# One trunk step on one core: a wider element stage in the RWKV layer, inverses of two head pairs together, and a memory projection in another place

## The chip, the cores and the metric

The kernel runs on one core of one Trainium2 chip. The metric is the device time of one execution in microseconds; the time before is the median of three runs. Its engines are called PE (matmuls; PEld is its weight loading), DVE and ACT (elementwise work that can also read PSUM, where matmul results land), POOL (elementwise work on SBUF only) and SP, whose queue issues nearly all of this kernel's transfers.

## The reference

One step of a two-layer network of width 1024 serves 512 prompt tokens and eight requests of 16 tokens. Layer 0 mixes by pooling and differential attention, layer 1 by RWKV; each is followed by cross attention to a memory of 256 rows and by a SwiGLU. What the change touches is in layer 1:

```python
    xr, xw, xk, xv, xa, xg = [h + xx * mu[i] for i in range(6)]
    r, k, v = xr @ wr, xk @ wk, xv @ wv
    a = jax.nn.sigmoid(a0 + (xa @ a1) @ a2)
    kk = heads(k * k_k)
    kk = kk / jnp.maximum(jnp.sqrt(jnp.sum(kk * kk, axis=-1, keepdims=True)), 1e-12)
    k = k * (1 + (a - 1) * k_a)
    decay = jnp.exp(-jnp.exp(w.astype(f32)))

    def step(S, inp):
        r_t, d_t, k_t, v_t, kk_t, a_t = inp
        sa = jnp.einsum('bhvk,bhk->bhv', S, -kk_t)
        S = (S * d_t[:, :, None, :] + sa[..., None] * (kk_t * a_t)[:, :, None, :]
             + v_t[..., None] * k_t[:, :, None, :])
        return S, jnp.einsum('bhvk,bhk->bhv', S, r_t)
```

Cross attention takes its keys and values from the memory, `mem_prompt @ xa_wk` and `mem_prompt @ xa_wv` (256 x 1024 each), which are also outputs.

## The kernel before, in words

All 640 tokens are columns (two halves of 320). Every large product is done in two-part arithmetic: an operand is split into a high part (a cast, mostly on ACT: `wh`, `split`) and a low part (a subtraction, on DVE or POOL: `wl`), and three matmuls are added. A product is a chain of steps, weights loaded by SP, cast, subtracted, multiplied, evicted from PSUM. Work is written in program order, and a scheduler then sets the order of each engine's instructions from its own estimates; on the chip each engine keeps its order and waits on semaphores. A tile with a tag lives in a ring of as many buffers as it was given, and the next user waits for the last one to be done with the buffer.

`rwkv` (layer 1) runs like this. Ahead of the keys, the memory's keys and values are made from `memhl`, the transposed memory in two parts (`mem_ksteps`, `mem_vsteps`); in the trace K is `p_g<-memhl,wh` and V is `p_g<-wh,memhl`. In the same time ACT, DVE and POOL make the mixed inputs (`mixed`: tiles `mixt`, `mixr`). Then come the key product (`kraw`, through `keep`), the low-rank inputs and the receptances.

The element stage goes over eight head pairs m, two heads on 128 partitions (`elem`, `rw_elem`). For each it makes: the decay's products (tiles `u`, `pi` and the views `P`, `S`); the normed key `kn`; `am`, the in-context rate and later the changed key; `zr`, the two left operands of each of ten chunks (eight of 64 prompt tokens, two of four requests each); `bk`, the two right operands per head, written over zeros in the other head's rows. From these PE makes the masked products `gm` of each chunk (`p_f<-zr,bk`), and transposes of bk (`p_f<-ident,bk`, copied out by ACT into `am`/`pi` tiles that go to DRAM as `d_bt`). zr, gm and their like go to DRAM (`d_w`, `d_gb`) through SP, to come back in another layout. While the head pairs run, pieces of a large product stand between their steps (`pace`: the rate is how many pieces per small PSUM tile; `rest` does all that is left): first the receptances, then the value product.

`inverse` makes, of each head pair, the inverse of a triangular 64 x 64 matrix per chunk: first the 16 x 16 blocks on the diagonal, by a loop of fifteen steps of a product and a sum on DVE (tiles `ix`, `in`, `it`), then a trip through DRAM (`d_np`), then two rounds of small PE products (`p_l`) to the matrix `mt`.

The chunk stage follows the string `CP`: `0` and `1` are the next chunk of the first and of the second half of the head pairs (pairs 0 to 3 and 4 to 7), `s` a sample part, `n` norms, `G` the gate's product, `Y` the last state. A chunk needs the state of the one ahead of it and the inverses of its four head pairs (`p_c<-u,mt`). Then come the gates, the output product, the cross attention of layer 1 (which reads K and V back from DRAM) and its SwiGLU.

## Time and profile before

| what | us |
|---|---|
| median of three runs (lowest, highest) | 2433.68 (2427.9, 2435.51) |
| span of the profiled execution | 2428.2 |
| layer 0, up to the memory projections | 0 to 1024 |
| memory K and V of layer 1, mixing | 1024 to 1096 |
| keys, low-rank inputs, receptances | 1096 to 1230 |
| element stage | 1230 to 1490 |
| chunk stage | 1490 to 1660 |
| norms, gates | 1660 to 1700 |
| output product, cross attention, SwiGLU, final norm | 1700 to 2428 |

The profile shows one execution. The span of 2428.2 us runs from the first to the last recorded instruction; the profiled execution's own time is not listed apart from it, and the median of the runs stands 5.5 us above. The stage borders were read from the first and last instructions of the tiles that belong to each. A row of a tile reads: line, engine, operation, output and inputs by the program's names, count, then shortest, median and longest duration in ns, then the first and last start. A row of a group has in their place the busy time and the mean duration, and, behind the bar, the idle time of the engine just before them and what ended it. A row of a window has its border and length, busy time and count for each engine, then the clock granted to PE as a share of full speed, the busy share of the DMA engines and the GB/s that they moved.

### The profile page before, as it was taken

Reading aid. Unit: us, or ns where it says so; the run is one execution under the profiler, and the core shown is the slowest. Engines: PE = TensorE matmul, PEld = TensorE weight load, DVE = VectorE, ACT = ScalarE, POOL = GpSimd, SP = SyncE. Lnnn points to the kernel's source line nnn. Section 1 sums busy time; section 2 is a strip of 40 time slices with the busy share of each in tenths; the row PEclk is TensorE's granted clock in tenths of the full one; section 3 lists DMA queues with packets and bytes.
Section 4 is the critical chain, followed back from the end, with each engine's and each line's share of the span. In section 5 each row is a group of like instructions: output and inputs, shape, how many; then the busy total and the mean of one; then the engine's idle time right before and its main releaser. Section 6 shows DMA issues by size and latency. Waiting matters only on the chain. (4 is left out here: it accounts for less than half of the span.)

```text
span 2428.2 us, 45754 instructions
## 1 busy us (share of the span) xinstructions
PE 2281.2 (94%) x18943; PEld 2119.8 (87%) x18943; DVE 1284.7 (53%) x2361; ACT 814.5 (34%) x1493; POOL 525.4 (22%) x536
## 2 busy tenths in 40 slices
PE   8998999999999999979998987696999999999998
PEld 7886999789999999978887876574997899999997
DVE  4467543454434424484759886579444544344344
ACT  4335432333212212366734432222323432122122
POOL 2122220012101102244555322233200212011010
PEclk9999999999999999999997878797999999999999
DMA  3218644423222222453245556674445222222222
GB/s 120 74 62 295 204 136 148 160 77 87 74 75 79 71 87 73 135 163 91 74 128 149 145 138 157 183 204 118 135 132 165 65 79 72 77 79 81 76 72 77
DMA packets 428322, 280.42 MB, mean 115 GB/s; under 512 B 79130, under 2 KB 383535, under 8 KB 428114
## 3 DMA queue, kind: packets, MB, share of 16 engines
q1 hardware_dynamic: 424513, 268.01, 38.0%
q0 software_dynamic: 3600, 9.49, 1.1%
q8 instruction: 149, 2.44, 0.4%
q14 instruction: 60, 0.48, 0.1%
HBM read 231.22 MB, written 46.20 MB: 114 GB/s over the span
## 5 line engine op out<-in xcount | busy, mean ns | idle before, releaser
L224 PE MATMUL p_g<-xn,wh 128*128 128x320 f32 x3712 | 721.6, 310 | 0.4 <-DVE xn L208 0.4
L224 PEld LDWEIGHTS p_g<-xn,wh 128*128 128x128 f32 x3712 | 588.7, 188 | 9.8 <-issue 8.4
L241 ACT CAST wh<-wr 128x1024 fp32r<-128x1024 f32 (+3 forms) x279 | 272.8, 978 | 861.7 <-PE p_g L224 534.0
L224 PE MATMUL p_g<-xn,wl 128*128 128x320 f32 x1856 | 444.1, 310 | 3.3 <-DVE wl L205 3.3
L205 DVE TENSOR_TENSOR wl<-wr,wh 128x1024 fp32r<-128x1024 f32 (+2 forms) x251 | 305.6, 1218 | 73.9 <-ACT wh L241 57.2
L224 PEld LDWEIGHTS p_g<-xn,wl 128*128 128x128 f32 x1856 | 316.2, 188 | 7.0 <-DVE wl L205 3.7
L224 PE MATMUL p_g<-hid,wh 128*128 128x320 f32 x1408 | 264.8, 309 | 0.0
L205 POOL TENSOR_TENSOR gate<-gate,sgate 128x320 f32<-128x320 f32 x88 | 118.1, 1363 | 676.1 <-DVE gate L205 517.6
L205 DVE TENSOR_TENSOR gate<-p_g,rstd 128x320 f32<-128x320 f32 x176 | 78.3, 486 | 327.5 <-PE p_g L224 324.8
L205 DVE TENSOR_TENSOR x<-x,p_g 128x320 f32<-128x320 f32 x192 | 85.5, 483 | 281.6 <-PE p_g L224 281.5
L224 PEld LDWEIGHTS p_g<-hid,wh 128*128 128x128 f32 x1408 | 221.4, 188 | 0.0
L224 PE MATMUL p_g<-hid,wl 128*128 128x320 f32 x704 | 161.4, 310 | 0.0
L224 PE MATMUL p_g<-mixr,wh 128*128 128x320 f32 (+2 forms) x640 | 128.4, 313 | 3.1 <-ACT wh L241 2.6
L224 PEld LDWEIGHTS p_g<-hid,wl 128*128 128x128 f32 x704 | 117.6, 188 | 0.0
L224 PE MATMUL p_g<-xohl,wh 128*128 128x320 f32 x512 | 110.0, 319 | 4.8 <-ACT xohl L214 4.7
L224 PEld LDWEIGHTS p_g<-mixr,wh 128*128 128x128 f32 (+2 forms) x640 | 98.5, 179 | 11.6 <-issue 5.6
L205 POOL TENSOR_TENSOR acc<-acc,sq 128x640 f32<-128x640 f32 x36 | 66.2, 1840 | 146.3 <-ACT sq L202 146.1
L224 PEld LDWEIGHTS p_g<-xohl,wh 128*128 128x128 f32 x512 | 82.4, 188 | 9.9 <-ACT xohl L214 7.0
L948 POOL TENSOR_SCALAR xp<-xp,xsm 128x256 f32<-128x256 f32 x32 | 15.3, 478 | 305.6 <-DVE xsm L684 299.6
L224 PE MATMUL p_g<-mixr,wl 128*128 128x320 f32 (+2 forms) x320 | 78.0, 314 | 0.0
L205 POOL TENSOR_TENSOR wl<-wr,wh 128x1024 fp32r<-128x1024 f32 (+2 forms) x28 | 64.4, 2301 | 60.4 <-ACT wh L241 57.2
L205 DVE TENSOR_TENSOR hid<-gate,hid 128x320 fp32r<-128x320 f32 x88 | 72.1, 819 | 7.8 <-ACT hid L214 7.8
(485 smaller groups left out, 3836.4 us busy)
## 6 DMA issues: line engine op xcount, KB each, us to landing
wr<-in_ffn_wg SPq DMA_DIRECT2D x44, 512.0 KB
wr<-in_ffn_wu SPq DMA_DIRECT2D x44, 512.0 KB
kc<-in_cache_mem_k SPq DMA_DIRECT2D x64, 256.0 KB
...
```

Of the source, the lines that this page charges most:

```text
L205: (eng or self.nc.vector).tensor_tensor(out, a, b, op=op)
L224: self.nc.tensor.matmul(out, lhsT, rhs, start=start, stop=stop, **kw)
L241: nc.scalar.copy(wh[0:rows, 0:n], wr[0:rows, 0:n])
L948: nc.gpsimd.tensor_scalar(p, p, rs, 1.0, op0=ALU.mult, op1=ALU.mult)
```

## The change

- Memory V of layer 1 (`mem_vsteps`) no longer stands behind K. It becomes the filler of the chunk stage (`K` at the head of `CP`, rate `KV` = 0.4), `memhl` is built a second time there from `mem_prompt`, and what is left at `G` is done ahead of the gate's product.
- `kn*am` and `am*k` and the `am` products of bk move from POOL to DVE. bk is one pair of tiles of 1280 columns, all ten chunks, in the place of three sets of halves; zr is two such tiles, and is made by four instructions in the place of eight, and stored by two transfers in the place of four.
- `inverse` takes two head pairs at once, after the second of them: its loop has the same thirty instructions for both. Its work tiles `iA` to `iE` have one buffer each and serve both phases. Of the last copies into `mt` two kinds change places between ACT and DVE.
- The low parts of the low-rank weights and `rn` get 128 rows, half of them zeros (`wz`, a tile of rn for each four pairs), where matmuls took 64 rows.
- Slots: 56 for 59; buffers of cached memory values in the cross attention: 8 for 9; POOL's ring of descriptors is smaller.

```diff
-NSLOT = 59
+NSLOT = 56
+BACC = dict(dynamic_dma_scratch_size=4096)
...
-    XV = 9
+    XV = 8
...
-    CP = '01s01sn01s01sn0101Gn01Y01n'
+    CP = 'K01s01sn01s01sn0101Gn01Y01n'
+    KV = 0.4
...
-            if m < 4:
-                rns.append(self.take(1, "rn", dt=F32R))
             a = 16 * m - 48
-            rn = rns[0][0][a:a + 64, 0:NT]
+            rns.append(self.take(1, "rn", dt=F32R))
+            rn = rns[-1][0][a:a + 64, 0:NT]
+            nc.gpsimd.memset(rns[-1][0][64 - a:128 - a, 0:NT].bitcast(F32), 0.0)
...
         with self.scope():
             self.all(self.mem_ksteps(1, self.mem))
-            self.all(self.mem_vsteps(1, self.mem))
         self.give(self.mem)
...
-            f = slice(64 * (m // 4), 64 * (m // 4) + 64)
-            yield from self.rw_elem(m, r, k, rns[0][0][f, 0:NT], selT[m % 4 // 2][0][f, c:c + 128], low_in, sp)
+            yield from self.rw_elem(m, r, k, rns[m // 4][0][:, 0:NT], selT[m % 4 // 2][0][:, c:c + 128], low_in, sp)
             if m < 4:
                 self.give(kr[0][m], kr[1][m])
-            inv[m] = self.inverse(m, sp, nsv[m // 4][:, m % 4])
+            if m % 2:
+                inv[m - 1:m + 1] = self.inverse(m - 1, sp, [nsv[i // 4][:, i % 4] for i in (m - 1, m)])
...
-        bks = self.take(6, "bk")
-        self.bk = [[t[:, 0:NT] for t in bks[2 * i:2 * i + 2]] for i in range(3)]
-        for b in self.bk:
-            for h in range(2):
-                nc.gpsimd.memset(b[h][64 - 64 * h:128 - 64 * h], 0.0)
+        self.bk = [self.wide(f"bk{h}", "bk") for h in range(2)]
+        for h in range(2):
+            nc.gpsimd.memset(self.bk[h][64 - 64 * h:128 - 64 * h], 0.0)
+        wzs = self.take(2, "wz", "n", dt=F32R)
+        self.wz = wzs
+        for t in wzs:
+            nc.gpsimd.memset(t[64:128, 0:128].bitcast(F32), 0.0)
+            nc.gpsimd.memset(t[0:64, 128:256].bitcast(F32), 0.0)
...
+            elif k == "K":
+                self.mem = self.mem_parts("x")
+                with self.inside(crings):
+                    self.pace(self.mem_vsteps(1, self.mem, self.take_tmp()), self.KV)
             elif k == "G":
+                self.rest()
+                self.give(self.mem, self.tmp)
...
-            r = slice(64 * i, 64 * i + 64)
             self.mm(p[:, 0:n], wa[:, i * 128:(i + 1) * 128], low[i][:, t0:t0 + n], start=True, stop=False)
-            self.mm(p[:, 0:n], wa[r, i * 128:(i + 1) * 128], low[2][r, t0:t0 + n], start=False, stop=True)
+            self.mm(p[:, 0:n], wz[:, i * 128:(i + 1) * 128], low[2][:, t0:t0 + n], start=False, stop=True)
...
-        zr = [self.t("zr", 3)[:, 0:NT].rearrange("p (c z t) -> p c z t", c=5, z=2) for _ in range(2)]
-        bk = [[t.rearrange("p (c z t) -> p c z t", c=5, z=2) for t in self.bk[(2 * m + i) % len(self.bk)]] for i in range(2)]
+        v = lambda t: t.rearrange("p (c z t) -> p c z t", c=10, z=2)
+        zr = v(self.wide(f"zr{m % 2}", "zr"))
+        bk = [v(t) for t in self.bk]
         yield
-        self.stt(zr[0][:, :, 0, :], ch(kn[:, 0:320]), -1.0, P[:, 0:5, 0:64])
-        self.stt(zr[1][:, 0:3, 0, :], ch(kn[:, 320:512]), -1.0, P[:, 5:8, 0:64])
-        self.tt(zr[0][:, :, 1, :], ch(r_[:, 0:320]), P[:, 0:5, 1:65])
-        self.tt(zr[1][:, 0:3, 1, :], ch(r_[:, 320:512]), P[:, 5:8, 1:65])
-        for i in range(2):
-            s = slice(512 + 64 * i, 576 + 64 * i)
-            self.stt(sq_(zr[1][:, 3 + i, 0, :]), sq_(kn[:, s]), -1.0, S[:, 4 * i:4 * i + 4, 0:16])
-            self.tt(sq_(zr[1][:, 3 + i, 1, :]), sq_(r_[:, s]), S[:, 4 * i:4 * i + 4, 1:17])
-        self.tt(kn, kn, am, eng=nc.gpsimd)
+        s4 = lambda t: t.rearrange("p (c s t) -> p c s t", c=2, t=16)
+        p4 = lambda t: t.rearrange("p (c s) t -> p c s t", c=2)
+        z4 = lambda z: zr[:, 8:10, z, :].rearrange("p c (s t) -> p c s t", t=16)
+        self.stt(zr[:, 0:8, 0, :], ch(kn[:, 0:512]), -1.0, P[:, :, 0:64])
+        self.tt(zr[:, 0:8, 1, :], ch(r_[:, 0:512]), P[:, :, 1:65])
+        self.stt(z4(0), s4(kn[:, 512:640]), -1.0, p4(S[:, :, 0:16]))
+        self.tt(z4(1), s4(r_[:, 512:640]), p4(S[:, :, 1:17]))
+        self.tt(kn, kn, am)
         self.act(am, am, AF.Identity, scale=c1("rw_k_a"), bias=self.ka1[:, m:m + 1])
-        self.tt(am, am, k, eng=nc.gpsimd)
-        for i in range(2):
-            for h in range(2):
-                r = slice(64 * h, 64 * h + 64)
-                s = slice(320 * i, 320 * i + 320)
-                self.tt(bk[i][h][r, :, h, :], ch(kn[r, s]), ch(pi[r, s]))
-                self.tt(bk[i][h][r, :, 1 - h, :], ch(am[r, s]), ch(pi[r, s]), eng=nc.gpsimd)
+        for h in range(2):
+            r = slice(64 * h, 64 * h + 64)
+            self.tt(bk[h][r, :, h, :], ch(kn[r]), ch(pi[r]))
+        self.tt(am, am, k)
+        for h in range(2):
+            r = slice(64 * h, 64 * h + 64)
+            self.tt(bk[h][r, :, 1 - h, :], ch(am[r]), ch(pi[r]))
...
-        for i in range(2):
-            for h in range(2):
-                nc.sync.dma_start(out=sp["w"][5 * i:5 * i + 5, hs(h), m, h, :].rearrange("c p f -> p c f"),
-                                  in_=zr[i][hs(h)].rearrange("p c z t -> p c (z t)"))
+        for h in range(2):
+            nc.sync.dma_start(out=sp["w"][:, hs(h), m, h, :].rearrange("c p f -> p c f"),
+                              in_=zr[hs(h)].rearrange("p c z t -> p c (z t)"))
...
-        X, N = [self.n(nm, self.IB[0])[0:nb] for nm in ("ix", "in")]
-        T = self.n("it", self.IB[1])[0:nb]
-        for b in range(8):
-            h, q = b // 4, b % 4
-            r = slice(64 * h + 16 * q, 64 * h + 16 * q + 16)
-            nc.sync.dma_start(out=X[b:nb:8].rearrange("c (s t) -> c s t", s=16), in_=sp["gb"][:, r, m, 16 * q:16 * q + 16])
+        w = [self.t(nm, 1)[:, 0:512] for nm in ("iA", "iB", "iC", "iD", "iE")]
+        X, N, T = [t[0:nb] for t in w[0:3]]
+        for i in range(2):
+            for b in range(8):
+                h, q = b // 4, b % 4
+                r = slice(64 * h + 16 * q, 64 * h + 16 * q + 16)
+                nc.sync.dma_start(out=X[b:nb:8, 256 * i:256 * i + 256].rearrange("c (s t) -> c s t", s=16),
+                                  in_=sp["gb"][:, r, m + i, 16 * q:16 * q + 16])
+        Xv = X.rearrange("p (i s t) -> p i s t", i=2, s=16)
+        Nv = N.rearrange("p (i s t) -> p i s t", i=2, s=16)
         nc.gpsimd.memset(N, 0.0)
-        nc.gpsimd.memset(N[:, 0:256:17], 1.0)
-        Xv = X.rearrange("p (s t) -> p s t", s=16)
-        Nv = N.rearrange("p (s t) -> p s t", s=16)
+        for i in range(2):
+            nc.gpsimd.memset(N[:, 256 * i:256 * i + 256:17], 1.0)
         for s in range(14, -1, -1):
             n = 15 - s
-            t = T[:, 0:n * n].rearrange("p (t j) -> p t j", t=n)
-            self.tt(t, Nv[:, s + 1:16, s + 1:16].rearrange("p j t -> p t j"), Xv[:, s, s + 1:16].unsqueeze(1).to_broadcast([nb, n, n]))
-            nc.vector.tensor_reduce(Nv[:, s, s + 1:16], t, axis=AX.X, op=ALU.add)
-        nc.sync.dma_start(out=sp["np"][m].rearrange("c b s t -> (c b) (s t)"), in_=N)
+            t = T[:, 0:2 * n * n].rearrange("p (i t j) -> p i t j", i=2, t=n)
+            self.tt(t, Nv[:, :, s + 1:16, s + 1:16].rearrange("p i j t -> p i t j"),
+                    Xv[:, :, s, s + 1:16].unsqueeze(2).to_broadcast([nb, 2, n, n]))
+            nc.vector.tensor_reduce(Nv[:, :, s, s + 1:16], t, axis=AX.X, op=ALU.add)
+        n16 = self.n("n16", 1)
+        gz, mts = [], []
+        for i in range(2):
+            nc.sync.dma_start(out=sp["np"][m + i].rearrange("c b s t -> (c b) (s t)"), in_=N[:, 256 * i:256 * i + 256])
+            nv = sp["np"][m + i].rearrange("c b s t -> (b s) c t")
+            nc.sync.dma_start(out=n16[:, 128 * i:128 * i + 128].rearrange("p (c t) -> p c t", c=8), in_=nv[:, 0:8])
+            nc.sync.dma_start(out=ns[i], in_=nv[:, 8:10])
+            gz.append(self.t("gz")[:, 0:512].rearrange("p (c t) -> p c t", c=8))
+            nc.sync.dma_start(out=gz[i], in_=sp["gb"][0:8, :, m + i, 0:64].rearrange("c p f -> p c f"))
+            mts.append(self.take(1, "mt"))
...
-        for h in range(2):
-            a, b_ = quads[2 * h], quads[2 * h + 1]
-            nc.scalar.copy(M[a, :, 0:32], ct(T)[a])
-            nc.gpsimd.memset(M[b_, :, 0:32], 0.0)
-            nc.vector.tensor_copy(M[b_, :, 32:64], ct(T)[b_])
-            nc.scalar.copy(M[a, :, 32:64], ct(p)[a])
-        mt[:] = [M]
-        return mt
+        for i in range(2):
+            M = mts[i][0][:, 0:512].rearrange("p (c t) -> p c t", c=8)
+            ci = lambda t: ct(t)[:, 8 * i:8 * i + 8]
+            for h in range(2):
+                a, b_ = quads[2 * h], quads[2 * h + 1]
+                nc.scalar.copy(M[a, :, 0:32], ci(T)[a])
+                nc.gpsimd.memset(M[b_, :, 0:32], 0.0)
+                nc.scalar.copy(M[b_, :, 32:64], ci(T)[b_])
+                nc.vector.tensor_copy(M[a, :, 32:64], ci(p)[a])
+            mts[i][:] = [M]
+        return mts
```

What moved in the engines' orders, at three places. DVE ahead of the first key copy (`kraw`); before:

```order
L205 TENSOR_TENSOR mixr<-mixt,mixr 128x640
L205 TENSOR_TENSOR wl<-wr,wh 128x1024
L205 TENSOR_TENSOR mixr<-mixt,mixr 128x640
L205 TENSOR_TENSOR wl<-wr,wh 128x1024
L194 COPY mv<-p_g 128x256
L205 TENSOR_TENSOR wl<-wr,wh 128x1024
L208 SCALAR_TENSOR_TENSOR mixt<-h,ct,mixt 128x512
L208 SCALAR_TENSOR_TENSOR mixt<-h,ct,mixt 128x128
L194 COPY mv<-p_g 128x256
L208 SCALAR_TENSOR_TENSOR mixt<-h,ct,mixt 128x512
L208 SCALAR_TENSOR_TENSOR mixt<-h,ct,mixt 128x128
L194 COPY kraw<-p_g 128x320 x2
```

and after:

```order
L216 TENSOR_TENSOR mixr<-mixt,mixr 128x640
L219 SCALAR_TENSOR_TENSOR mixt<-h,ct,mixt 128x512
L219 SCALAR_TENSOR_TENSOR mixt<-h,ct,mixt 128x128
L219 SCALAR_TENSOR_TENSOR mixt<-h,ct,mixt 128x512
L216 TENSOR_TENSOR mixr<-mixt,mixr 128x640
L219 SCALAR_TENSOR_TENSOR mixt<-h,ct,mixt 128x128
L219 SCALAR_TENSOR_TENSOR mixt<-h,ct,mixt 128x512
L219 SCALAR_TENSOR_TENSOR mixt<-h,ct,mixt 128x128
L216 TENSOR_TENSOR mixr<-mixt,mixr 128x640
L205 COPY kraw<-p_g 128x320 x2
```

V's low parts `wl` and copies `mv` are gone from between the mixing instructions, and the key copies follow at the eighth `mixr`.

DVE at the second head pair, before (POOL does `kn<-kn,am`, `am<-am,kraw` and `bk<-am,pi` in between):

```order
L208 SCALAR_TENSOR_TENSOR kn<-kraw,ct,p_e 128x320
L208 SCALAR_TENSOR_TENSOR zr<-kn,u 128x5x64
L194 COPY krst<-p_g 128x320
L208 SCALAR_TENSOR_TENSOR kn<-kraw,ct,p_e 128x320
L208 SCALAR_TENSOR_TENSOR zr<-kn,u 128x3x64
L208 SCALAR_TENSOR_TENSOR zr<-kn,u 128x64 x2
L205 TENSOR_TENSOR bk<-kn,pi 64x5x64 x4
L208 SCALAR_TENSOR_TENSOR kn<-kraw,ct,am 128x640
L194 COPY krst<-p_g 128x320
L205 TENSOR_TENSOR gm<-p_f,mask_p 128x512
```

and after:

```order
L219 SCALAR_TENSOR_TENSOR zr<-kn,u 128x2x64
L216 TENSOR_TENSOR kn<-kn,am 128x640
L1519 COPY bon<-p_f 128x10
L216 TENSOR_TENSOR am<-am,kraw 128x640
L216 TENSOR_TENSOR gm<-p_f,mask_p 128x512 x2
L205 COPY krst<-p_g 128x320
L216 TENSOR_TENSOR gm<-p_f,mask_p 128x512 x2
L216 TENSOR_TENSOR gm<-p_f,mask_s 128x256 x2
L205 COPY krst<-p_g 128x320
L216 TENSOR_TENSOR bk<-kn,pi 64x10x64 x2
L216 TENSOR_TENSOR bk<-am,pi 64x10x64 x2
L219 SCALAR_TENSOR_TENSOR kn<-kraw,ct,am 128x640
```

The products of POOL stand on DVE now, and bk is written behind the masks `gm` of the pair ahead of it, whose products and transposes read the same two tiles.

PE at the last inverse, before (`p_l` are the inverse's products of pair 7, here 16 or 32 of 32x32 in a row, `p_c_16949` the first half's third chunk, `p_c_16380` the first chunk of the second half):

```order
L224 MATMUL p_l<-iNT,gz 32x32 x32
L224 MATMUL p_c_16927<-tr,wc 64x64
L224 MATMUL p_y_16938<-tr,wc 64x64
L224 MATMUL p_c_16927<-tr,wc 64x64 x7
L224 MATMUL p_y_16938<-tr,wc 64x64 x7
L224 MATMUL p_y_16938<-tr,ident 64x256
L224 MATMUL p_l<-iN,iY 32x32 x32
L224 MATMUL p_y_16938<-tr,ident 64x256
L224 MATMUL p_c_16949<-u,mt 64x64 x8
L224 MATMUL p_l<-iNT,gz 32x32 x16
L224 MATMUL p_l<-iT,iY 32x32 x16
L224 MATMUL p_c_16380<-u,mt 64x64 x2
```

and after (`p_l` serves pairs 6 and 7; `p_c_16565` is the first half's third chunk, `p_c_15887` the second half's first):

```order
L235 MATMUL p_y_16144<-tr,gbc 64x64 x8
L235 MATMUL p_c_16531<-tr,wc 64x64 x7
L235 MATMUL p_y_16542<-tr,wc 64x64 x8
L235 MATMUL p_y_16542<-tr,ident 64x256 x2
L235 MATMUL p_c_16565<-u,mt 64x64 x8
L235 MATMUL p_l<-iB,gz 32x32 x64
L235 MATMUL p_l<-iD,iA 32x32 x64
L235 MATMUL p_l<-iB,gz 32x32 x32
L235 MATMUL p_l<-iE,iA 32x32 x32
L235 MATMUL p_c_15887<-u,mt 64x64 x3
L232 MATMUL p_x<-ident,mt 128x128 x2
L235 MATMUL p_c_15887<-u,mt 64x64
```

The last inverse stands at the first half's third chunk in both orders. Before it was pair 7's alone, and pairs 4 to 6 had gone into the second half's first chunk already; now it is that of pairs 6 and 7, four times as many products in a row, and memory transposes (`p_x<-ident,mt`) and V follow.

56 lines of the change are left out of this document (28 added, 28 removed).

## The prediction

> **What bounds the kernel now.** I read the page's first part, then the busy time by stage, then the groups of DVE and POOL in the element stage, then single tiles. From the page and the stages:
>
> ```profile
> span 2428.2 us, 45754 instructions
> PE 2281.2 (94%) x18943; PEld 2119.8 (87%) x18943; DVE 1284.7 (53%) x2361; ACT 814.5 (34%) x1493; POOL 525.4 (22%) x536
> core 0: us, PE busy (x) PEld busy (x) DVE busy (x) ACT busy (x) POOL busy (x), PEclk, DMA share, GB/s
> ...
> 1024.00:1096.00 72.00, 59.30 (x452) 55.76 (x451) 59.78 (x98) 46.44 (x77) 29.72 (x39) 0.93 0.55 167
> 1096.00:1230.00 134.00, 131.08 (x817) 114.99 (x816) 76.32 (x92) 85.97 (x154) 67.60 (x48) 1.00 0.29 82
> 1230.00:1490.00 260.00, 229.53 (x2688) 198.88 (x2686) 211.49 (x479) 98.34 (x211) 108.67 (x127) 0.86 0.56 142
> 1490.00:1660.00 170.00, 136.61 (x2422) 107.56 (x2422) 107.92 (x247) 44.12 (x110) 38.11 (x35) 0.83 0.71 197
> 1700.00:2428.00 728.00, 711.07 (x5055) 690.21 (x5053) 311.34 (x487) 200.43 (x335) 89.13 (x73) 0.99 0.31 93
> ```
>
> PE is 94% busy over the span, and in the last row it carries the time at full clock. In 1230 to 1490, the element stage, its clock is 0.86 and its matmuls are small, while DVE is busy 81% of the time: there I take DVE for the bound, with PE close behind. The change touches the memory projections (1024 to 1096), the element stage and the chunks (1490 to 1660), 500 us in all. I sum against this execution's span; the median of the runs, 2433.7, lies 5.5 us above it, and I lay that on at the end. About 0.3% (7 us) is what a measurement of this kernel tells from no change.
>
> **Term 1: memory V leaves the place ahead of the keys.** Tiles memhl and mixr, one window, and V's low parts on DVE:
>
> ```profile
> L224 PEld LDWEIGHTS p_g<-memhl,wh x128: 187/188/337, 1024.0 to 1060.9; 128*128 128x128 f32 x128
> L224 PEld LDWEIGHTS p_g<-wh,memhl x128: 186/188/337, 1061.3 to 1095.2; 128*128 128x128 f32 x128
> 1061.00:1096.00 35.00, 27.74 (x203) 26.63 (x202) 26.50 (x35) 22.25 (x37) 13.63 (x17) 0.90 0.63 190
> L224 PEld LDWEIGHTS p_g<-mixr,wh x54: 186/188/189, 1095.5 to 1110.0; 128*128 128x128 f32 x54
> L194 DVE COPY kraw<-p_g x8: 476/492/493, 1106.2 to 1228.6; 128x320 f32<-128x320 f32 x8
> L214 ACT CAST mixr<-mixt x16: 708/726/733, 1047.6 to 1103.7; 128x640 fp32r<-128x640 f32 x16
> L205 DVE TENSOR_TENSOR wl<-wr,wh 128x1024 fp32r<-128x1024 f32 x8 | 10.2, 1278 | 5.6 <-ACT wh L241 5.6
> ```
>
> K is done at 1061, V (weights wh on the left) fills the 34 us to 1095.2, and the keys' first weights follow at 1095.5 (their first copy out, kraw, at 1106.2). Without V the keys start when K is done and the first eight mixed operands are there. Sixteen casts run from 1047.6 to 1103.7, so the eighth stands at 1047.6 + 7 x 56.1/15 = 1073.8, its low part two microseconds later; DVE's 10.2 us of V low parts are gone from between, which brings it forward again. I take 1073: **22 us gained**, with ends 15 (the old pace of mixing) and 34 (all of V). Late next is the mixing. The keys themselves are PE at clock 1.00 for 134 us and stay as they are.
>
> **Term 2: the element stage.** Groups and tiles in 1225 to 1540; the row that begins with 1225.00 is the busy time of the inverse's two loop instructions (tile it) on DVE and POOL:
>
> ```profile
> L205 DVE TENSOR_TENSOR bk<-kn,pi x32: 469/958/2673, 1241.8 to 1465.8; 64x320 f32<-64x320 f32 x32
> L205 DVE TENSOR_TENSOR bk<-kn,pi 64x320 f32<-64x320 f32 x32 | 30.1, 941 | 3.8 <-POOL kn L205 3.3
> L205 POOL TENSOR_TENSOR bk<-am,pi 64x320 f32<-64x320 f32 x32 | 33.4, 1045 | 2.4
> L205 POOL TENSOR_TENSOR kn<-kn,am 128x640 f32<-128x640 f32 x8 | 12.4, 1551 | 34.1 <-DVE zr L208 25.1 <-DVE in L1548 8.9
> L205 POOL TENSOR_TENSOR am<-am,kin 128x640 f32<-128x640 f32 x4 | 6.9, 1720 | 7.7 <-ACT am L202 6.3 <-DMA d_bt<-am 1.5
> L205 POOL TENSOR_TENSOR am<-am,kraw 128x640 f32<-128x640 f32 x4 | 6.5, 1626 | 3.8 <-ACT am L202 2.9 <-POOL mt L1598 1.0
> L205 POOL TENSOR_TENSOR wl<-wr,wh 128x1024 fp32r<-128x1024 f32 x12 | 28.5, 2374 | 27.3 <-ACT wh L241 27.0
> L205 POOL TENSOR_TENSOR mixr<-krst,mixr 128x640 fp32r<-128x640 f32 x4 | 8.3, 2066 | 2.6 <-ACT mixr L214 2.5
> L205 DVE TENSOR_TENSOR mixr<-mixt,mixr x8: 804/812/1852, 1052.2 to 1086.2; 128x640 fp32r<-128x640 f32 x8
> 1225.00:1540.00 315.00, 77.59 (x240) 0.00 (x0) 0.82 0.59 149
> L1548 DVE TENSOR_REDUCE in<-it 80x1 f32<-80x1 f32 x8 | 1.2, 146 | 0.2
> L205 DVE TENSOR_TENSOR it<-in,ix 80x49 f32<-80x49 f32 x8 | 4.6, 576 | 0.2
> L205 DVE TENSOR_TENSOR it<-in,ix 80x36 f32<-80x36 f32 x8 | 1.6, 206 | 0.1
> L205 DVE TENSOR_TENSOR gm<-p_f,mask_s x16: 402/424/425, 1257.0 to 1485.7; 128x256 f32<-128x256 f32 x16
> ```
>
> First what these rows say beside their sizes. The product bk takes 469 ns at its shortest and 958 at the median; a 49-element step of the inverse takes 576 in the mean where a 36-element one takes 206; gm, which reads PSUM, stays at 402 to 425. So DVE instructions that read two SBUF operands are being held up, in this window by mean less shortest of each form 61 us in all: bk has 32 x (941 - 469) ns = 15.1 of it, the other forms 46. POOL runs its own two-operand products at the time, 33.4 + 12.4 + 6.9 + 6.5 = 59.2 us that the change takes away and 28.5 + 8.3 = 36.8 that it leaves. DVE work of the stage, then, over eight pairs (a one-element instruction, 146 ns, is the fixed price of one):
>
> - bk: 32 instructions of 64x640 in the place of 32 of 64x320, at the 0.81 us of a free 128x640 product (mixr's median): 25.9 for 30.1, -4.2.
> - The two products kn, am that come over from POOL: 16 x 0.81 = +13.0.
> - zr in four instructions a pair for eight: 32 x 0.146 = -4.7.
> - The inverse's loop for two pairs at once: 240 become 120, 120 x 0.146 = -17.5 of 77.6. Its seven other DVE instructions a pair are halved too: 28 x 0.146 = -4.1. The copies into mt are four a pair before and after, two of each kind having changed engines: 0.
> - The hold-up of the other forms shrinks with what POOL still does: 46 x 59.2/96 = 28; new DVE instructions meet what is left, so -24 (ends 0, if it has another cause, and -46).
>
> Sum -41.5 on DVE, ends -17 and -64. A rule of the Trainium skill speaks here ("SBUF — State Buffer", Who interferes with whom): a DVE instruction with two SBUF inputs and a GpSimd instruction that reads SBUF exclude each other for a whole instruction. The trace agrees in kind (958 against 469 ns, and gm from PSUM untouched). By that rule each microsecond of POOL's 59.2 is one in which DVE could not start such a product, and the DVE term would be nearer -64 than -41.
>
> Not all of it reaches the clock. bk had three half sets and now has one, so that the next pair's bk, in DVE's order, waits for this pair's transposes from it, with everything that stands behind it on DVE (bonus, masks gm, the next zr). The bounds and SP's queue:
>
> ```profile
> L1524 PE MATMUL p_f<-ident,bk x160: 213/225/367, 1256.4 to 1487.4; 64*128 64x64 f32 x160
> L1501 SPq DMA_DIRECT2D d_w<-zr x32: 575/626/791, 1233.8 to 1461.8; - x32
> L1514 SPq DMA_DIRECT2D d_gb<-gm x48: 574/575/2124, 1248.2 to 1486.1; - x48
> L1515 SPq DMA_DIRECT2D d_w<-gm x48: 597/614/1767, 1248.9 to 1486.7; - x48
> ```
>
> Twenty transposes a pair are at most 20 x 0.225 = 4.5 us behind its last gm, for seven pairs 31; nothing if the masks and transposes of one pair are over before the next bk is due. I take 13 in between, since DVE has the two-pair inverse and the mixing to set there. SP's queue runs nearly all DMAs: these rows alone are 128 issues, some 77 us of 260. zr's are halved (-16 x 0.63 = -10 us), so SP is no worse; it isn't the first bound but caps the gain. The zero rows that make 64-row weights 128 rows, two extra ACT copies a pair and one more memset of rn cost nothing: ACT is at 98 of 260 us, POOL loses 59; without that cover they'd be some 5 us. So **28 us gained** (ends 0 and 55).
>
> **Term 3: the chunks.** V's work arrives here, as filler between chunk steps: PE 27.5 us (nearly all of the 27.74 above), DVE 10.2 and as much again for copies and the rebuilt memhl, 12 loads (5 MB; at the stage's 197 GB/s 27 us of transfer time, where the DMA engines are at 0.71). PE is at 136.6 of 170, so it has 33 us of gaps to take it; on the path I put +5. The gates now stand behind all of V. The other part is the tail of the inverses:
>
> ```profile
> L1548 DVE TENSOR_REDUCE in<-it x20: 142/264/383, 1489.8 to 1513.4; 80x11 f32<-80x121 f32 x2, 80x12 f32<-80x144 f32 x2, 80x13 f32<-80x169 f32 x2, 80x14 f32<-80x196 f32 x2
> L1549 SPq DMA_DIRECT2D d_np<-in x2: 447/484/522, 1493.9 to 1517.4; - x2
> L1600 ACT COPY mt<-p_l x6: 361/362/363, 1490.4 to 1536.6; 32x256 f32<-32x256 f32 x6
> L1695 ACT COPY yl<-p_y x16: 362/372/392, 1498.6 to 1661.4; 128x256 f32<-128x256 f32 x16
> ```
>
> Now the last gm ends at 1486, pair 7's loop at 1513.8, and its matrix is there at 1536.6, when the second half of the heads can start its chain: 50 us behind the last gm, 23 of them from loop to matrix. A two-pair loop is 2 x 77.6/8 - 30 x 0.146 = 15 us, with 23 behind it 38. In the new order pairs 4 and 5 start at the last gm, and the five work tiles have one buffer each, so pairs 6 and 7 follow after: 76 us for 50. In both orders PE comes to the last inverse at the first half's third chunk, so that half runs on in between and leaves the engines freer later: I put +10 of the 26 on the end. **15 us lost**, ends -5 and +65.
>
> The smaller edits (one vc buffer fewer, three slots fewer, a smaller descriptor ring) I count at zero: PE is 98% busy in the stage of the cross attention; without that slack +3 for each layer.
>
> Sum: -22 - 28 + 15 = -35 on 2428.2, that is 2393, and with 5.5 for the median **2399**; its own range 2384 to 2416.
>
> **Rivals.**
> - *DVE's whole relief reaches the clock*: the hold-up ends for all forms, DVE falls by up to 64, 50 of it in the stage's length: -22 - 50 + 10 = -62, 2372. For it: DVE at 81%, POOL's bk beside it; against it: PE at 0.86 clock and one bk set. 0.20.
> - *The bound only passes on*: PE, SP's queue and the wait for bk hold the element stage at 255: -22 - 5 + 15 = -12, 2422, hardly faster, and no change if term 1 comes at its lower end. For it: PE busy 229.5 of 260. 0.17.
> - *Slower*: the second half's chain is the end of the stage and nothing is given back: 26 us later for the inverses, and each of its eight prompt chunks (sixteen yl copies for both halves, the last 125 us after the last mt) waits behind an eighth of V, 3.4 us, and 1.6 us for its loads: 26 + 8 x 5 = 66. Then -22 - 26 + 66 = +18, 2452. It decides from a chunk stage of 220 us. For it: DMA at 0.71 and gates behind V; against: 33 us of PE gaps. 0.15.
> - The forecast: 0.48.
>
> Faster than 2426: the forecast, the first rival and half of the second, 0.76; within 0.3%: 0.09; slower 0.15. The range takes in most of the first rival and all of the second: 2364 to 2436.
>
> **What would show it.** Term 1: keys' first copy near 1084 instead of 1106. Term 2: bk on DVE near 0.81 us without a tail of 2 us, its idle time before bk ended by PE; the last gm 45 to 55 us earlier. Term 3: the last mt copy some 76 us behind the last gm, the last yl copy 120 us behind that. Wrong it would be if bk keeps its stretched median, or if the last chunk ends over 200 us after the last gm.

## The result: 30 us slower

The changed kernel takes 2462.1 us in the median (2458.4 to 2469.1, four runs) against 2432.0 for the kernel before beside it: ratio 1.0127, 95% interval 1.0108 to 1.0146. Forecast were 2399 us, with a range of 2364 to 2436. The profiled execution's span is 2460.9 us, 32.7 above the one before. From the page and from single tiles of the kernel after:

```profile
span 2460.9 us, 45633 instructions
PE 2288.7 (93%) x18959; PEld 2126.9 (86%) x18959; DVE 1272.0 (52%) x2205; ACT 822.0 (33%) x1509; POOL 468.6 (19%) x486
...
L205 DVE COPY kraw<-p_g x8: 477/491/492, 1087.7 to 1218.9; 128x320 f32<-128x320 f32 x8
L216 DVE TENSOR_TENSOR gm<-p_f,mask_p x32: 672/680/693, 1235.8 to 1447.4; 128x512 f32<-128x512 f32 x32
L216 DVE TENSOR_TENSOR gm<-p_f,mask_s x16: 402/416/426, 1241.2 to 1449.6; 128x256 f32<-128x256 f32 x16
L1630 DVE COPY mt<-p_l x16: 411/418/423, 1354.8 to 1540.9; 32x256 f32<-32x256 f32 x16
L1725 ACT COPY yl<-p_y x16: 354/372/385, 1475.9 to 1703.7; 128x256 f32<-128x256 f32 x16
L235 PE MATMUL p_g<-glhl,wh x48: 304/355/636, 1671.6 to 1714.1; 128*128 128x320 f32 x32, 96*128 96x320 f32 x16
```

The layer's path is cut at five places: the first key copy (kraw), the first and the last masked product (gm), the last matrix of the inverses (mt), the last chunk's copy (yl). Their start times tell where the time went. Such rows of every run give this table (us between the starts; the first column is the start of the first kraw, the last but one what the span holds behind the last yl). Each row is one profiled execution, and that can lie up to 7 us from the run's median (e12 7 above it, e17 7 below), so the medians in the text decide on times and the table only says where they went:

| run | first kraw | to first gm | gm, first to last | last gm to last mt | last mt to last yl | to the end | span |
|---|---|---|---|---|---|---|---|
| before | 1106.2 | 141.3 | 238.2 | 50.9 | 124.8 | 766.8 | 2428.2 |
| after | 1087.7 | 148.1 | 213.8 | 91.3 | 162.8 | 757.2 | 2460.9 |
| e1 V ahead of the keys | 1108.4 | 145.6 | 217.4 | 87.9 | 121.8 | 762.1 | 2443.2 |
| e2 single inverses | 1088.7 | 151.4 | 216.2 | 66.9 | 163.6 | 756.7 | 2443.5 |
| e3 both of these | 1109.0 | 149.9 | 236.0 | 54.1 | 130.7 | 759.3 | 2439.0 |
| e4 before, V moved | 1081.9 | 143.3 | 236.1 | 47.4 | 171.4 | 759.1 | 2439.2 |
| e5 as e1, two sets of tiles | 1127.7 | 140.8 | 210.8 | 63.4 | 121.3 | 765.2 | 2429.2 |
| e6 as e1, last four single | 1106.5 | 148.3 | 223.2 | 61.9 | 128.3 | 752.1 | 2420.3 |
| e7 as e1, products on POOL | 1104.9 | 145.9 | 224.5 | 86.2 | 128.2 | 755.0 | 2444.7 |
| e8 as e1, iA by POOL's queue | 1107.0 | 145.9 | 194.3 | 119.7 | 119.7 | 760.9 | 2447.5 |
| e9 before, two-pair inverse | 1107.4 | 149.5 | 212.8 | 94.0 | 116.2 | 772.6 | 2452.5 |
| e10 before, last four single | 1104.9 | 148.1 | 233.7 | 42.3 | 118.1 | 771.0 | 2418.1 |
| e11 as e6, d_bt by ACT | 1105.6 | 148.4 | 190.4 | 90.8 | 117.6 | 761.3 | 2414.1 |
| e12 as e10, d_bt by ACT | 1108.2 | 149.5 | 218.6 | 63.7 | 127.6 | 760.4 | 2428.0 |
| e13 before, d_bt by ACT | 1105.8 | 141.4 | 225.8 | 71.6 | 121.2 | 763.2 | 2429.0 |
| e14 as e4, rate 1.2 | 1081.8 | 144.8 | 235.6 | 53.0 | 165.6 | 759.2 | 2440.0 |
| e15 as e3, d_bt by ACT | 1111.0 | 150.8 | 209.8 | 77.0 | 130.5 | 755.0 | 2434.1 |
| e16 as e4, gates first | 1084.5 | 144.9 | 240.7 | 62.2 | 124.1 | 775.0 | 2431.4 |
| e17 as e11, more buffers | 1106.7 | 147.1 | 194.9 | 87.1 | 121.6 | 757.4 | 2414.8 |
| e18 as e10, V behind gates | 1084.0 | 142.2 | 227.0 | 63.9 | 120.6 | 785.2 | 2422.9 |

After against before: -18.5 at the keys, +6.8 to the first gm, -24.4 in the element stage, +40.4 from the last gm to the last mt, +38.0 from there to the last yl, -9.6 behind it; the sum is +32.7. The front of the change gains 36 us by the last gm, where 45 to 55 were forecast; the chunk stage gives back 78.

The chunk stage in slices of 20 us, of the kernel after and then of the kernel before (columns: PE, PEld, DVE, ACT, POOL busy, clock, DMA share, GB/s):

```profile
1480.00:1500.00 20.00, 16.82 (x318) 13.64 (x318) 7.37 (x15) 8.32 (x18) 2.96 (x5) 0.57 0.62 149
1500.00:1520.00 20.00, 0.00 (x0) 0.00 (x0) 13.95 (x34) 0.00 (x0) 2.34 (x2) 0.51 0.28 70
1520.00:1540.00 20.00, 8.22 (x384) 7.50 (x384) 4.53 (x9) 4.37 (x10) 0.00 (x0) 0.50 0.21 40
1540.00:1560.00 20.00, 19.86 (x182) 16.32 (x182) 7.66 (x17) 4.75 (x12) 0.00 (x0) 0.79 0.45 138
1560.00:1580.00 20.00, 20.00 (x309) 17.17 (x308) 14.64 (x30) 7.32 (x15) 5.90 (x9) 1.00 0.80 244
1580.00:1600.00 20.00, 20.00 (x197) 13.52 (x195) 9.05 (x13) 4.06 (x10) 6.57 (x7) 1.00 0.54 146
1600.00:1620.00 20.00, 20.00 (x289) 15.16 (x285) 14.04 (x31) 3.81 (x9) 5.45 (x6) 1.00 0.74 211
```

```profile
1520.00:1540.00 20.00, 12.68 (x274) 9.76 (x274) 8.05 (x22) 6.22 (x14) 2.16 (x3) 0.61 0.80 212
1540.00:1560.00 20.00, 12.17 (x211) 10.37 (x211) 9.11 (x17) 4.22 (x9) 4.67 (x4) 0.62 0.62 180
1600.00:1620.00 20.00, 19.25 (x311) 15.39 (x307) 17.23 (x35) 6.53 (x17) 5.25 (x4) 0.92 0.59 148
1620.00:1640.00 20.00, 19.79 (x286) 15.32 (x286) 12.04 (x27) 5.73 (x14) 7.25 (x7) 1.00 0.86 238
1640.00:1660.00 20.00, 18.69 (x386) 14.76 (x380) 16.55 (x34) 6.73 (x17) 5.30 (x5) 1.00 0.82 247
```

After: PE does nothing at all from 1500 to 1520, and is then full for three slices, with V among the chunks. Before, PE's gaps lay in the same early place, and from 1600 on it was 96% busy (57.73 of 60). In the waits of PE in 1450 to 1545, and in the loads of the loop's input iA there (the first column of the second row is the line of the DMA issue):

```profile
PE p_l L235 <- issue: 32.0, 3, 28.4
L1561 SPq DMA_DIRECT2D iA<-d_gb x20: 739/739/1384, 1439.3 to 1504.4; - x20
L235 PE MATMUL p_l<-iE,iA x128: 236/236/256, 1488.9 to 1539.3; 32*32 32x32 f32 x128
L1616 ACT COPY iA<-p_l x4: 577/578/578, 1486.5 to 1537.0; 32x512 f32<-32x512 f32 x4
```

The inverse of pairs 4 and 5 uses iA until its last products (1488.9 on). Only then can SP load pairs 6 and 7 into it, sixteen issues of 0.74 us, the last at 1504.4; their loop follows, and PE, whose next instruction is this inverse's product, stands for 28.4 us.

### The profile page after: what moved, and what is told of

The parts are those of the page before. It is cut to its first block, busy times and chain, and to the rows that moved or that the text cites. A ratio compares the mean times of both kernels' runs of the same rounds, so it can differ in the third digit from the quotient of the medians.

```text
span 2460.9 us, 45633 instructions
## 1 busy us (share of the span) xinstructions
PE 2288.7 (93%) x18959; PEld 2126.9 (86%) x18959; DVE 1272.0 (52%) x2205; ACT 822.0 (33%) x1509; POOL 468.6 (19%) x486
## 5 line engine op out<-in xcount | busy, mean ns | idle before, releaser
L252 ACT CAST wh<-wr 128x1024 fp32r<-128x1024 f32 (+2 forms) x279 | 272.7, 979 | 851.4 <-PE p_g L235 527.3
L216 POOL TENSOR_TENSOR gate<-gate,sgate 128x320 f32<-128x320 f32 x88 | 118.1, 1364 | 728.5 <-DVE gate L216 728.5
L235 PE MATMUL p_g<-mixr,wh 128*128 128x320 f32 (+2 forms) x640 | 134.9, 321 | 8.2 <-ACT lowx L213 3.0
L216 DVE TENSOR_TENSOR hid<-gate,hid 128x320 fp32r<-128x320 f32 x88 | 71.6, 814 | 9.1 <-ACT hid L225 9.1
```

The source lines that it names most:

```text
L216: (eng or self.nc.vector).tensor_tensor(out, a, b, op=op)
L235: self.nc.tensor.matmul(out, lhsT, rhs, start=start, stop=stop, **kw)
L252: nc.scalar.copy(wh[0:rows, 0:n], wr[0:rows, 0:n])
```

## The experiments

Diffs are against the kernel named; line ends are cut.

**e1 to e4: which part costs what.** e1 puts V back (after, minus the `K` step):

```diff
-    CP = 'K01s01sn01s01sn0101Gn01Y01n'
+    CP = '01s01sn01s01sn0101Gn01Y01n'
             self.all(self.mem_ksteps(1, self.mem))
+            self.all(self.mem_vsteps(1, self.mem))
```

> The changed kernel with memory V back behind K, ahead of the keys; all else as changed. Theory A (two losses in the chunk stage: the inverse of pairs 6 and 7 ends 91 us behind the last gm where it was 51, and V then lengthens the second half's chain from 125 to 163 us): the chain from the last mt to the last yl goes back to about 125 us (-38), the first key copy goes back by 18 us, so 2442 us. Rival B (all of the 78 us is V: its loads in SP's queue, its transposes ahead of the first chunk on PE): the last mt also comes back to some 50 us behind the last gm, 2400. Rival C (all is the inverses): 2462 + 18 = 2480.

2441.1 us, 1.0050 (1.0030 to 1.0069) of before. Theory A's 2442, and each of its places: mt to yl is back at 121.8, the first kraw at 1108.4, while the last mt stays 88 us behind the last gm. B and C fall.

e2 takes the inverse of the kernel before, one pair at a time, into the changed kernel (`inv[m] = self.inverse(m, sp, nsv[m // 4][:, m % 4])`); V stays in the chunk stage.

> The changed kernel with the inverse of one head pair at a time as before; V stays in the chunk stage. Theory A: the last mt comes back to 50 to 60 us behind the last gm (-35), the element stage pays some 10 for 17 us more of DVE work, 2437. Rival B (all V): nothing gained at the tail, the element stage longer, 2470. Rival C (all is the inverses): 2462 - 78 + 10 = 2394.

2444.4, 1.0060 (1.0043 to 1.0077): between A and B, the last mt at 66.9 instead of 55, V's 163.6 unchanged.

e3 does both.

> Both undone: V ahead of the keys and the inverse of one pair at a time, so that what is left of the change is the wide b, k, z on DVE, the zero rows and the smaller pools. Theory A: -38 - 35 + 18 + 10 on 2462, that is 2417, some 15 us below the kernel before. If the wide element stage gives nothing by itself: 2432.

2446.2, 1.0068 (1.0049 to 1.0087), above either alone and above the kernel before. A's sum fails: undoing the two parts doesn't add up, for here the element stage is 236.0, where it was 217.4 and 216.2 with either of them. What is left of the change, the wide b, k, z with the zero rows and the smaller pools, takes 2 us from the stage (238.2 before) and makes the whole run slower. Why e2, with single inverses too, has a stage 20 us shorter than this run isn't shown: the two differ only in where V stands.

e4 is the kernel before with V moved as in the change.

> The kernel before with one edit: memory V as the filler of the chunk stage, with memhl built a second time. Theory A: 18 us gained at the keys, 38 lost in the chunks, 2432 + 20 = 2452. Rival D (V only hurts because PE stands idle at the two-pair inverse first, and hides in the gaps that the old chunk stage leaves on PE): 2415 to 2425.

2444.3, 1.0058 (1.0039 to 1.0076). 24 us gained at the keys, 47 lost behind the last mt. V costs without any change of the inverse, so rival D falls; A's 2452 was too high by 8.

**e5 and e6: the tail of the inverses.** e5 is e1 with two buffers for the loop's tiles:

```diff
-NSLOT = 56
-NHALF = 22
+NSLOT = 58
+NHALF = 17
-        w = [self.t(nm, 1)[:, 0:512] for nm in ("iA", "iB", "iC", "iD", "iE")]
+        w = [self.t(nm, n)[:, 0:512] for nm, n in (("iA", 2), ("iB", 2), ("iC", 2), ("iD", 1), ("iE", 1))]
```

> Memory V ahead of the keys, two-pair inverses as changed, and two buffers each for the loop's tiles iA, iB and iC (iD, iE one each), with 58 and 17 slots of the two sizes. Beside the run with V put back alone (span 2443.2, last mt 88 us behind the last gm): if the single set is what puts the last inverse behind that of pairs 4 and 5, its loads and its loop start before those are through, the last mt stands 55 to 65 us behind the last gm, and the time is 2412 to 2422. Rival (the place of the inverse in DVE's and SP's order is what decides, not the buffers): within 5 us of 2443.

2427.0, 0.9974 (0.9962 to 0.9986). The last mt comes from 88 to 63 us behind the last gm, within what was expected of the buffers: the single set was a large part of it. The first kraw is 19 us later than in e1, ahead of anything that uses these tiles: probably the five small slots taken away cost that elsewhere, and then the time understates the step; no run took them away alone.

e6 is e1 with the old inverse for pairs 4 to 7:

```diff
-            if m % 2:
+            if m > 3:
+                inv[m] = self.inverse1(m, sp, nsv[m // 4][:, m % 4])
+            elif m % 2:
                 inv[m - 1:m + 1] = self.inverse(m - 1, sp, ...
```

> Memory V ahead of the keys; pairs 0 to 3 in two-pair inverses, pairs 4 to 7 one at a time as before. If the two-pair form is worth its DVE time in the element stage and costs only at the tail: element stage some 10 us shorter than with single inverses alone (236), last mt 50 to 58 us behind the last gm, 2420 to 2428. Rival (the single form costs the element stage so much that only its end counts): 2440 or more, as with both undone.

2422.0, 0.9946 (0.9927 to 0.9964), the time expected. The stage is 223.2 us, 13 below e3's, and the last mt stands 61.9 behind the last gm, where 50 to 58 were expected.

**e7 to e9: what shortened the element stage.** e7 puts `kn*am`, `am*k` and bk's am products of e1 back on POOL.

> Memory V ahead of the keys, two-pair inverses, but kn*am, am*k and the am products of bk back on POOL in their wide form. If POOL's two-operand products hold up DVE's (as the prediction's hold-up term has it): bk<-kn,pi rises from 1.2 us mean to 1.6 or more, DVE's stage gets 10 us longer, 2450 to 2460. If DVE is not the bound of the stage: within 5 us of 2443, and the hold-up costs nothing.

2448.4, 1.0067 (1.0047 to 1.0086), just between the two cases. The stage is 7 us longer than e1's, where the first case had 10. Tile bk, of e7 and of e1:

```profile
L216 DVE TENSOR_TENSOR bk<-kn,pi x16: 804/822/3009, 1216.9 to 1461.1; 64x640 f32<-64x640 f32 x16
L216 POOL TENSOR_TENSOR bk<-am,pi x16: 1524/2020/3001, 1225.3 to 1459.2; 64x640 f32<-64x640 f32 x16
```

```profile
L216 DVE TENSOR_TENSOR bk<-kn,pi x16: 775/820/2904, 1219.6 to 1450.7; 64x640 f32<-64x640 f32 x16
L216 DVE TENSOR_TENSOR bk<-am,pi x16: 804/819/3021, 1227.5 to 1451.5; 64x640 f32<-64x640 f32 x16
```

DVE's product has the same median and the same longest time in both, but the mean of bk from kn is 1433 ns in e7 for 1151 in e1 (1.6 us or more was expected): 7 of 16 took over 1 us in place of 3. In e1, which leaves POOL the subtractions `wl` and the mixing, five of the 32 bk products took over 2 us and the others at most 0.82; each of the five ran beside a `wl` or a `mixr` of POOL. Two of them, on DVE, and POOL at the same time (start and duration in us):

```profile
1380.91 2.86 DVE L216 TENSOR_TENSOR bk<-kn,pi 64x640 f32<-64x640 f32 x1 [0.26 <-PE p_f L1544]
1383.69 3.02 DVE L216 TENSOR_TENSOR bk<-am,pi 64x640 f32<-64x640 f32 x1
1380.70 5.33 POOL L216 TENSOR_TENSOR wl<-wr,wh 128x1024 fp32r<-128x1024 f32 x2 [5.49 <-ACT wh L252]
```

So POOL's products do hold DVE's up, as the prediction said, and the few that are left keep the tail of 3 us. Whether that is what lengthens e7's stage isn't shown: DVE is busy in it for 155.8 us, less than the 161.6 of e1, since the products are POOL's again. The move of the products was worth 7 us.

e8 has the sixteen iA loads of each two-pair inverse of e1 issued by POOL's queue.

> Memory V ahead of the keys, two-pair inverses, the sixteen loads of the loop's input iA issued by POOL's queue in the place of SP's (0.74 us each there, 47 us of SP over the layer). If SP's queue bounds the element stage and the 13 us of loads ahead of the last loop count at the tail: element stage 10 us shorter, last mt 75 us behind the last gm, 2420 to 2430. If SP is no bound: within 5 us of 2443, or longer where POOL's issue is slower.

2444.3, 1.0048 (1.0029 to 1.0067), no gain. The stage is 23 us shorter, and the last mt stands 32 us further behind it. It doesn't tell SP's part from that of loops that moved behind the last gm.

e9 is the kernel before with the two-pair inverse alone (64 slots, the smaller ring).

> The kernel before with one edit, the inverse of two pairs at a time (64 slots and the smaller descriptor ring, so that its five tiles find room); narrow bk and zr, POOL's products and V as before. If the two-pair inverse is what shortened the element stage (214 to 218 us with it, 236 without, whether b, k, z are wide or not): first to last gm 217 to 222 us, last mt 85 to 90 us behind the last gm, so 2431 - 18 + 37 - 5 = 2445. If the wide b, k, z on DVE are needed for it: 236, and 2460.

2453.8, 1.0077 (1.0059 to 1.0094). 212.8 us in the element stage with narrow b, k, z: the two-pair inverse alone shortens it by 25 us, as much as the whole change. Its 120 loop instructions add up to 52 us on DVE, the 240 of the single ones to 77.6. But the last mt stands 94 us behind the last gm, so from the first gm to the last mt it is 306.8 us for 289.1, and by itself that inverse loses more than it gains. Each of the three parts alone is slower than the kernel before: the wide form with the smaller edits 1.0068 (e3), the two-pair inverse 1.0077, V 1.0058 (e4). Together they lose 1.0127, less than the sum of the three.

**e10 to e13, e15: what else bounds the stage.** e10 is the kernel before with two-pair inverses for pairs 0 to 3.

> The kernel before with two-pair inverses for pairs 0 to 3 and single ones for pairs 4 to 7. If the wide b, k, z on DVE are worth nothing or cost a little (the run with both undone is 15 us above the kernel before): faster than the same with them (2422), 2408 to 2418. If they are worth their DVE time: 2425 to 2432.

2417.3, 0.9930 (0.9914 to 0.9945), as expected if the wide form is worth nothing here. It is 4.8 us below e6, the same with wide b, k, z, but the intervals of the two overlap. The gain against the kernel before sits behind the last gm (42.3 and 118.1 us) rather than in the stage (233.7).

e11 is e6 with one line's queue changed:

```diff
-            nc.sync.dma_start(out=sp["bt"][c0:c0 + nch, :, m, :]...
+            nc.scalar.dma_start(out=sp["bt"][c0:c0 + nch, :, m, :]...
```

> The run with V ahead of the keys and single inverses for pairs 4 to 7 (2422), with the 24 stores of bk's transposes (d_bt) issued by ACT's queue, right behind the ACT copies that make them, in the place of SP's. If SP's queue, 189 of 236 us in instructions of its own with both undone, bounds the element stage: 8 to 12 us less from first to last gm, 2412. If it is no bound: within 4 us of 2422, a little longer where ACT pays for the issues.

2417.1, 0.9930 (0.9915 to 0.9944), and the stage falls from 223.2 to 190.4, three times what was expected. The idle time before instructions of tile am that ended with the store's landing, of e6 and of e11:

```profile
  DMA d_bt<-am: 33.7, 11
```

```profile
  DMA d_bt<-am: 13.7, 8
```

ACT's copies had waited until the stores of their buffers, issued by SP, had landed; over half of that wait is gone. But the last mt comes 91 us behind the last gm, and only 5 us reach it and the time (intervals that overlap e6's): the inverses end the stage now. The line also gives these stores a DMA queue of their own (9296 packets of it from 1260 to 1440 us); whether that helps, or that SP's order no longer holds them, no run separates.

e12 (e10 with that line) and e13 (the kernel before with it) ask what the narrow form gains.

> The kernel before with the inverses of pairs 0 to 3 two at a time (2417) and the 24 stores of d_bt on ACT's queue. In the kernel with wide b, k, z the same stores took the first to last gm from 224 to 191 us. If SP's queue is the bound for the narrow form too: 234 to 205 or less here, and 2405 to 2413 since the inverses end the stage then. If the narrow form is held by DVE and POOL instead (so that the wide form pays once the queue is relieved): 225 or more, 2414 to 2418.

> The kernel before with that one edit, the d_bt stores on ACT's queue; single inverses, narrow b, k, z, V as before. If SP's queue is the first bound of the element stage: 239 us falls to 215 or less, 2415 to 2425. If DVE is: within 5 us of 239, 2426 to 2436.

2422.5, 0.9961 (0.9947 to 0.9975), and 2429.3, 0.9986 (0.9972 to 0.9999). The stage falls by 15 and by 12 us, less than 234 to 205 and 239 to 215; the last mt moves by 11 and 8 us the other way. e12 is 5 us slower than e10 without the line, above both of its cases: for the narrow form with two-pair inverses the line is a loss (their intervals don't overlap). The stores in SP's queue are one bound of the narrow form's stage; that they aren't the first is argued from the size alone.

e15 is e3 with the line, the wide form without the two-pair inverse.

> The run with both undone (wide b, k, z on DVE, single inverses, V ahead of the keys; 236 us from first to last gm, 2446) with the 24 stores of d_bt on ACT's queue. The narrow form went from 239 to 226 us by the same step. If SP's queue hid what the wide form takes off DVE and POOL: 236 falls by more than the narrow form's 12, to 215 or less. If the wide form gives DVE nothing: 224 to 230. The time follows only in part, since the last inverses then end the stage: 2425 to 2440.

2432.2, 1.0005 (0.9991 to 1.0019). 236.0 falls to 209.8, 26 us where the narrow form had 12. So the wide form is worth some 14 to 16 us of the stage once the stores are out of SP's queue, and 2 with them in it. A part of that is work that moved: 90 of the 240 loop instructions of the inverses now stand behind the last gm, where e3 had 53. In the profiled executions the last mt stays where it was (1548.6, in e3 1549.0) and the span falls by 5 us; by the medians the run is 14 us faster than e3 (2446.2), of whose four executions the profiled one was the fastest.

e17 gives e11's single inverses a second buffer each for their input and result (ix, in) and for the tiles n16 and gz behind the loop (IB = 2, 1, 2, 2 for four ones).

> The run with V ahead of the keys, single inverses for pairs 4 to 7 and d_bt on ACT's queue (2417; last mt 91 us behind the last gm), with two buffers each for the single inverses' input, matrix, and their copies (ix, in, n16, gz in the ring). If the single buffers keep the four last inverses apart: last mt 60 to 70 us behind the last gm, 2400 to 2410. If their place in DVE's order does: within 4 us of 2417.

2423.4, 0.9957 (0.9939 to 0.9974), and 87 us behind the last gm: no gain, and above both cases. The loops do come earlier with these buffers, the last sum of a loop starting at 1475.4 where it was 1494.8 in e11, but the last mt doesn't (1535.8, 1535.2). What holds it there stands behind the loops, among the loads, products and copies that lead to mt; which of them isn't shown.

**e14, e16, e18: V.** e14 is e4 with `KV = 1.2`.

> The kernel before with V moved to the chunks, as in the run at rate 0.4 (2444; last mt to last yl 171 us), but at rate 1.2, so that V stands on PE ahead of the second half's first chunk. If V costs because it comes when PE is full (96% busy behind the last mt) and its gaps lie ahead of that: 125 to 140 us behind the last mt, 2420 to 2432. If V's loads or the gates behind it cost: 160 or more, 2440 to 2450.

2438.3, 1.0022 (1.0009 to 1.0035), and the chain from mt to yl is 165.6 for 171.4. V is done 36 us earlier than in e4, and the gates' product (`p_g<-glhl,wh`) is nearly as late as there (e4's rows stand below, with e16):

```profile
L225 PE MATMUL p_g<-glhl,wh x48: 304/412/637, 1648.3 to 1687.4; 128*128 128x320 f32 x32, 96*128 96x320 f32 x16
L225 PE MATMUL p_g<-wh,memhl x256: 274/281/388, 277.4 to 1571.3; 128*128 128x256 f32 x128
```

So V's place in PE's order is a small part of its cost.

e16 is e4 with the gates first:

```diff
-    CP = 'K01s01sn01s01sn0101Gn01Y01n'
+    CP = 'G01s01sn01s01snK0101n01Y01n'
             elif k == "K":
+                self.rest()
+                self.give(glh)
```

> The kernel before with V moved to the chunks, but with the gates' product as the first filler (where it was) and V begun only behind it, late in the chunk stage; what is left of V is done ahead of the norms and gates. If V costs by holding back the gates (their inputs were loaded at 1641 and their product ran from 1648 in the runs with V first, from 1560 before): last mt to last yl 140 us or less, 2420 to 2432. If V's PE work and loads in that stage cost by themselves, wherever: 2438 to 2448.

2428.0, 0.9979 (0.9965 to 0.9993): 16 us below e4, with the same V in the same stage, and mt to yl is 124.1. The gates' product and V, of e4 and of e16:

```profile
L225 PE MATMUL p_g<-glhl,wh x48: 302/313/636, 1652.6 to 1689.1; 128*128 128x320 f32 x32, 96*128 96x320 f32 x16
L225 PE MATMUL p_g<-wh,memhl x256: 274/281/580, 279.2 to 1606.9; 128*128 128x256 f32 x128
```

```profile
L225 PE MATMUL p_g<-glhl,wh x48: 304/412/637, 1481.6 to 1530.7; 128*128 128x320 f32 x32, 96*128 96x320 f32 x16
L225 PE MATMUL p_g<-wh,memhl x256: 274/281/581, 280.0 to 1693.8; 128*128 128x256 f32 x128
```

With V first the gates' inputs come into slots that V held, and their product runs at the very end. With the gates first they run in the early gaps, V after them; 8 us come back behind the last yl (775.0 for 766.8), where V now ends. The run doesn't only undo the delay: the kernel before has its gates' product at 1560 to 1639, and here it is 78 us ahead of that. No run moved the gates alone.

e18 puts e10 and e16 together.

> The kernel before with what paid: two-pair inverses for pairs 0 to 3, single ones for 4 to 7 (2417 by itself), and V behind the gates in the chunk stage (2428 by itself, against 2433). If the two add up: 2417 - 4 = 2413, the first key copy near 1083, last mt to last yl 125 us. If V takes the gaps that the hybrid's chunk stage (118 us) has already used: 2420 to 2428.

2423.4, 0.9954 (0.9937 to 0.9972). They don't add up: against e10 the first key copy comes 21 us earlier, but the last mt stands 22 us further behind the last gm (63.9 for 42.3), and 14 us more lie behind the last yl (785.2 for 771.0). e10 and e11, 2417 us and 0.9930 of before, stay the fastest.

## Why the prediction was wrong, step by step

The step that failed is term 3: it put +15 into the sum for the chunk stage, and +78 was measured there (10 of which come back behind the last yl), because neither the wait for the last inverse nor V was covered by other work as it assumed. Terms 1 and 2 together gave 36 us of their 50, term 2 for a wrong reason.

- *Term 1, V away from the keys, 22 us.* 18.5 at the first key copy (24 in e4). Right, though forecast at 1084 it came at 1087.7; 7 us of it go until the first gm. Why is open: e9 and e10, with narrow b, k, z, have 149.5 and 148.1 us there too, e4 has 143.3.
- *Term 2, the element stage, 28 us.* 24.4 measured, and that it came so near is luck, for its own step "DVE is the bound" failed. The busy times from the first to the last gm, of the kernel before and of e3, which has the wide form without the two-pair inverse (columns: PE, PEld, DVE, ACT, POOL busy):

```profile
1248.00:1486.00 238.00, 208.26 (x2493) 180.32 (x2491) 196.85 (x453) 90.22 (x196) 95.81 (x112) 0.84 0.57 143
1259.00:1495.00 236.00, 189.53 (x2474) 171.01 (x2472) 182.98 (x427) 90.78 (x201) 48.45 (x69) 0.86 0.58 149
```

The wide form takes 14 us of work off DVE (some 20 of the -41.5 were its share), and the stage is 2 us shorter. The two-pair inverse, -21.6 in the sum, shortens it by 25 us alone (e9). What the wide form is worth, 14 to 16 us, appears when its stores leave SP's queue (e15 against e13). "It isn't the first bound but caps the gain" was said of SP on the strength of 128 issues, 77 us; all 280 of its issues between the first and the last gm of the kernel before add up to 181 us of 238. It should have been a term.
- *The hold-up, -24.* The direction was right: by the same reckoning, mean less shortest of each form, 17 us of it are left in e3. But the 61 us seem to count bk twice. Over the rows of the kernel before, all such forms together come to 46 us with bk's 15.1 among them, so the other forms have 31, and the term would have been some -16.
- *The bk set, 13 us.* Nearly nothing as a wait: in the groups of the kernel after, DVE's idle time just before bk is 1.5 us. What the order costs that puts bk behind the masks, no run tells.

```profile
L216 DVE TENSOR_TENSOR bk<-kn,pi 64x640 f32<-64x640 f32 x16 | 20.0, 1252 | 1.2 <-PE p_f L1545 0.9
L216 DVE TENSOR_TENSOR bk<-am,pi 64x640 f32<-64x640 f32 x16 | 13.1, 817 | 0.3
```

- *Price of the wide products, 0.81 us.* 0.82 at the median; the tail of 2.9 us, which was to vanish, stayed, so the mean of bk from kn is 1.25 us. POOL's remaining `wl` and `mixr` keep it (e7).
- *Term 3, the inverses, +10 of 26.* 40.4. The wait was sized at 76 us behind the last gm and measured 91.3: left out were the sixteen loads of iA in SP's queue, which can't be issued before the buffer is free (13 us); with two sets it is 63.4 (e5). And only 10 of the 26 us were put on the end, since PE reaches this inverse at the first half's third chunk in both orders. That was read as cover; but PE keeps its order, the inverse's product was next in it, and PE stood for 28.4 us.
- *Term 3, V, +5.* 38.0. "33 us of gaps" was an average of the stage. The gaps lay in 1500 to 1560, when V had hardly begun, and behind 1600 PE was 96% busy. That the gates "now stand behind all of V" was written down and not priced. e14 and e16 point to it as most of V's loss: with V done early and the gates still late the chain is 165.6 us, with the gates ahead of V 124.1. It isn't isolated, since e16 also moves V behind and the gates ahead of their old place.
- *The rivals.* The slower one named this mechanism and nearly this size (26 for the inverses and 40 for V, 2452 with a point of decision at a chunk stage of 220 us; it became 254 from last gm to last yl) and got 0.15. For the inverses the trace bore it out better than that: this half followed from the order and from rows that were shown. For V its size was right by luck, because it let every chunk wait for an eighth of V and for its loads, and in e14, with V done at 1571, the chain is hardly shorter.

Not settled: why e10's tail is shorter than the kernel's before (42.3 for 50.9), why the last mt stays at 1535 to 1549 when the stores leave SP's queue and the last gm comes earlier (in e11 the loops are through 40 us ahead of it, in e6 18 us), why V's place changes the element stage by 20 us in the wide form with single inverses (e2, e3), and where the 9.6 us behind the last yl come from, for which the sum had nothing. No run undid the zero rows, the smaller pools or the vc buffer by themselves.
